# Order of the attention heads of the first half in an encoder layer: block by block, or the pairs of two blocks alternating

## Chip, cores and metric

The kernel runs on one core of a Trainium2 chip, in one launch. The metric is the time of one execution on the device in microseconds (us), as the median of several runs. The engines are named TensorE (PE in the rows; PEld is its weight load), VectorE (DVE), ScalarE (ACT), GpSimd (POOL) and SyncE (SP), whose queue starts nearly all DMA transfers here.

## The reference

One layer over 2048 positions of 1024 channels, all in float32:

```python
h = rms_norm(x, norm_mix_g[l])
z = h @ w_in[l]                      # u_a, v_a, q_b, k_b, v_b, f_logit
out_a = spatial_gating(u_a, v_a, ...)        # 8 heads, GELU and a layernorm per head
out_b = forgetting_attention(q_b, k_b, v_b, f_logit)   # 8 heads of 64
x = x + concatenate([out_a, out_b], -1) @ w_out[l]
x = x + conv_ffn(rms_norm(x, norm_ffn_g[l]), ...)
return rms_norm(x, norm_final_g)
```

`forgetting_attention` is causal: for head h and query t it takes `softmax(q k^T / 8 + c[t] - c[s])` over the keys s <= t, with c a running sum of log-sigmoids, and multiplies by v.

## The kernel before

The 2048 positions are four blocks of 512 queries, `tb` 0 to 3; blocks 0 and 1 are the first half. Every product is made in three matmuls from high and low parts of its operands (`mm3`, lines 180 to 192).

The order of the stages is: projections of the first half (`a_half(0)`: keys and queries, values, then `gated`, which has a layernorm stage of eight tiles and a gate stage of eight tiles, each tile 24 matmuls of `mm3`), projections of the second half (`a_half(1)`: the two `gated` stages first, then values, then keys and queries), the output projection of the first half (`c_half`), its feed-forward part (`d_half`), and the second half (`late_half`).

Attention is no stage of its own. It is a generator, `b_stream` (line 623), that takes a list of pieces (head, block) and makes them in that order. A piece has two parts. `b_max` (line 666) loads the queries t1 and t2, makes the scores of 128 queries against up to 512 keys in two matmuls (L686, L687), takes their row minimum (scores are stored negated) on VectorE (L690 for full blocks, L692 with the mask for the block on the diagonal), and the exponential with its sum on ScalarE (L695); it ends with the reciprocal of the sum (L714, or L716 in block 0). `b_mix` (line 726) makes the transposed scores (L747, L748), the mask (L751, diagonal only), the exponential (L753), a high and a low part of it (L758, L759) and the product with the values (L735, L736); it ends with L770 and L771, and after the second head of a pair the sums are turned to rows (L776), multiplied in and stored to `mixh[tb]` and `mixl[tb]` in DRAM (L782 to L785). `b_stream` runs the maxima of piece p+1 before the mixing of piece p. The score tiles are three banks in turn.

Every `yield` of the generator is one step. In block 0 `b_max` has 4 steps and `b_mix` 4, plus 2 that drain the last products, plus one in every odd head; in block 1 it is 8 and 8, plus the same. `start_fill` (line 464) starts the stream as the first half's values are done. `tick` (line 83), called after each matmul of a projection, adds 1 to a credit and makes one step for each 3.5 ticks in the first half, 4.0 in the second (`RATES`). Instructions of the stream are given a higher priority than what stands around them, and a list scheduler that knows estimated durations fixes each engine's final order when the program is built; each engine then runs its queue in order. Blocks 2 and 3 begin only when `self.ready` is set, after `phase_a`.

`need(tb)` (line 116) makes steps at once, without matmuls of a projection in between, until block `tb` is complete. `need(0)` stands in `a_half(1)` (line 430), after the first block's queries, ahead of `load_mix(0)`, which loads what attention and the gates of block 0 left in `mixh[0]` and `mixl[0]`; `need(1)` stands in `c_half` (line 810).

Of the kernel before, what the change touches and what calls it, by code (L numbers as in the profile page):

```python
# [31 lines left out]
RATES = [3.5, 4.0, 4.4, 3.6]  # L32
# [36 lines left out]
class Block:  # L69
# [45 lines left out]

    def need(self, tb):

        while self.done < 8 * (tb + 1):
            self.step()
            self.count += 3  # L120
            while self.late and self.late[0][0] <= self.count:
                self.late.pop(0)[2]()
# [262 lines left out]
    def a_half(self, half):  # L385
# [28 lines left out]
        def keys_queries():  # L414
            u0, u1 = self.first if half == 0 else (self.a_unit("k", 0), self.a_unit("k", 1))
            self.a_forget(half, 0)
            channels("k", 0, *u0, 0)
            channels("k", 1, *u1, 0)
            self.a_forget(half, 1)
            channels("k", 0, *u0, 1)  # L420
            channels("k", 1, *u1, 1)
            groups = (("k", (2, 3)), ("q", (0, 1)), ("q", (2, 3))) if half == 0 else (("k", (2, 3)), ("q", (0, 1, 2, 3)))
            for kind, cs in groups:
                with self.tc.issue_after(self.rows_ins), self.tc.issue_after(self.pow_ins):
                    us = [(c, self.a_unit(kind, c)) for c in cs]
                for b in range(2):
                    for c, u in us:
                        channels(kind, c, *u, b)
                    if half == 1 and kind == "q" and b == 0:
                        self.need(0)  # L430
                        self.mix0 = self.load_mix(0)

            if half == 0:
                with self.tc.issue_after(self.raw_ins):
                    self.a_gate_w(sp, pp)
                    self.scales = [self.a_rows(1, b, False) for b in range(2)]

        def values():
            for t, ps in token_major(2048):
                pv = ps.rearrange("p (h d) -> p h d", h=8)  # L440
                hl = self.til(sp, [P, 2, 8, 64], F32R, "vn")
                hi, lo = hl[:, 0, :, :], hl[:, 1, :, :]
                nc.scalar.activation(hi, pv, AF.Copy)
                nc.vector.tensor_tensor(lo, pv, f32(hi), op=ALU.subtract)
                self.dma(self.vd[half][t * P:(t + 1) * P, :, 0:64], f32(hi))
                self.dma(self.vd[half][t * P:(t + 1) * P, :, 64:128], f32(lo))

        def gated():
            vns = []
            for t, ps in token_major(512):  # L450
                if t % 2 == 0:
                    vns.append(self.til(sp, [P, 2, TB], F32, "vn"))
                self.a_layernorm(ps, vns[-1][:, t % 2, :])
            for t, ps in token_major(0):
                if t % 2 == 0:
                    self.a_mixed(vns[t // 2])
                self.a_gate(half * 2 + t // 4, t % 4, ps, vns[t // 2][:, t % 2, :])
                if half == 0 and t % 4 == 3:
                    self.a_norm(1, t // 4, self.scales[t // 4], 14 if t == 3 else 16, 9 if t == 3 else 6)

        if half == 0:
            keys_queries()
            values()
            self.start_fill(self.b_stream([(h, tb) for tb in range(4) for h in range(8)]), RATES[0])
            gated()
        else:
            self.rate = RATES[1]
            gated()
            values()
            keys_queries()  # L470
# [934 lines left out]
```

## Time and profile before

| | |
|---|---|
| median of 3 runs | 2499.26 us (2495.81 to 2500.54) |
| profiled execution, its own time | 2500.66 us |
| its span, first to last instruction | 2499.0 us |
| TensorE busy in the span | 2438.5 us, 98% |
| VectorE busy | 1743.9 us, 70% |
| ScalarE busy | 1365.2 us, 55% |
| GpSimd busy | 344.3 us, 14% |
| granted TensorE clock, mean | 0.995 of full speed |

The rows come from one profiled execution. Busy time is the time in which at least one instruction of an engine ran. An idle time is put down to the engine or transfer whose event ended it; of several events, to the last.

### The profile page before, as it was taken

To read this page: it belongs to the slowest core of one execution; us is meant where nothing else is said; L and a number is where in the kernel's file an instruction comes from. 1 tells how busy PE (TensorE), PEld (TensorE's weight loads), DVE (VectorE), ACT (ScalarE), POOL (GpSimd) and SP (SyncE) were. 2 spreads that over 40 slices of the span, in tenths; PEclk is the share of its full clock that TensorE was granted. 3 is DMA by queue.
4 is the path that set the end of the run, shared out by engine and by line. 5 is a ranking of instruction groups with operands and counts; after the bars stand their busy time and mean duration, and the time that the engine had idled before them with its cause. 6 is when DMAs were issued, how large, how long until landed. Compare 5 with 4: busy or idle time off the path is not lost.

```text
span 2499.0 us, 32991 instructions
## 1 busy us (share of the span) xinstructions
PE 2438.5 (98%) x11082; PEld 1995.1 (80%) x11082; DVE 1743.9 (70%) x3106; ACT 1365.2 (55%) x2629; POOL 344.3 (14%) x351
## 2 busy tenths in 40 slices
PE   8999989999999999999999999999999999999998
PEld 5787867878788888887888888878888887888887
DVE  5237667655457867887777875488788887857776
ACT  4327767654345556766676772255555545444443
POOL 3214122000014221121111121120000000001000
PEclk9999999999999999999999999999999999999999
DMA  6863543666857545554555545512222228538633
GB/s 181 260 165 101 160 120 113 186 163 179 281 186 239 161 144 167 185 173 154 170 160 154 180 154 197 165 43 93 81 80 82 84 80 299 168 102 293 196 119 122
DMA packets 346101, 396.08 MB, mean 158 GB/s; under 512 B 52908, under 2 KB 222068, under 8 KB 344508
## 3 DMA queue, kind: packets, MB, share of 16 engines
q1 hardware_dynamic: 340892, 369.85, 48.3%
q0 software_dynamic: 5040, 24.12, 2.5%
q8 instruction: 88, 1.44, 0.3%
q14 instruction: 81, 0.66, 0.1%
HBM read 300.30 MB, written 93.72 MB: 158 GB/s over the span
## 4 chain that ended last, share of the span: by engine, by line
PE 83%; DVE 5%; DMA 4%; ACT 4%; issue 2%; POOL 1%; SPq 1%; DVEq 0%; POOLq 0%; ACTq 0%
PE D L1271 15%; PE mm L188 12%; PE mm L190 12%; PE mm L192 12%; PE A L1085 3%; PE A L1084 3%; PE A L1086 3%; PE o L736 2%; PE o L735 2%; PE s L687 2%; PE s L686 2%; PE s L748 2%; PE s L747 2%; PE B L1084 2%; PE B L1085 2%
## 5 line engine op out<-in xcount | busy, mean ns | idle before, releaser
L188 PE MATMUL mm<-thi,whi 128*128 128x512 f32 x960 | 377.5, 393 | 2.7 <-DVE vn L398 2.7
L192 PE MATMUL mm<-thi,wlo 128*128 128x512 f32 x960 | 377.0, 393 | 0.1
L190 PE MATMUL mm<-tlo,whi 128*128 128x512 f32 x960 | 376.5, 392 | 0.0
L188 PE MATMUL mm<-whi,thi 128*128 128x512 f32 x640 | 253.5, 399 | 4.7 <-DVE m L704 1.1
L190 PE MATMUL mm<-wlo,thi 128*128 128x512 f32 x640 | 254.2, 397 | 1.8 <-DVE wlo L142 1.7
L192 PE MATMUL mm<-whi,tlo 128*128 128x512 f32 x640 | 252.9, 396 | 0.0
L130 POOL TENSOR_SCALAR whi<-raw 128x1024 fp32r<-128x1024 f32 x108 | 125.2, 1160 | 916.8 <-PE mm L190 514.2
L695 ACT ACTIVATE s<-s,part 128x512 f32<-128x512 f32 (+3 forms) x257 | 150.4, 585 | 147.5 <-DVE part L690 83.0
L188 PEld LDWEIGHTS mm<-thi,whi 128*128 128x128 f32 x960 | 180.5, 188 | 41.1 <-DVE vn L398 2.9
L192 PEld LDWEIGHTS mm<-thi,wlo 128*128 128x128 f32 x960 | 180.5, 188 | 38.4 <-DVE wlo L142 0.6
L190 PEld LDWEIGHTS mm<-tlo,whi 128*128 128x128 f32 x960 | 180.5, 188 | 37.2
L759 DVE TENSOR_TENSOR pl<-e,ph 128x512 fp32r<-128x512 f32 (+2 forms) x212 | 138.1, 658 | 62.2 <-ACT ph L758 34.4
L142 DVE TENSOR_TENSOR wlo<-raw,whi 128x1024 fp32r<-128x1024 f32 x108 | 135.2, 1253 | 47.6 <-POOL whi L130 47.3
L753 ACT ACTIVATE e<-s 128x512 f32<-128x512 f32 (+2 forms) x227 | 115.5, 528 | 72.4 <-DVE s L751 41.5
L188 PEld LDWEIGHTS mm<-whi,thi 128*128 128x128 f32 x640 | 121.4, 190 | 30.4 <-POOL whi L130 3.3
L190 PEld LDWEIGHTS mm<-wlo,thi 128*128 128x128 f32 x640 | 121.4, 190 | 27.1 <-DVE wlo L142 4.2
L1271 PE MATMUL D<-wl,xh 128*128 128x512 f32 x368 | 141.2, 389 | 0.0
L1271 PE MATMUL D<-wh,xh 128*128 128x512 f32 x368 | 140.8, 389 | 0.2 <-DVE xo L1343 0.2
L192 PEld LDWEIGHTS mm<-whi,tlo 128*128 128x128 f32 x640 | 121.2, 190 | 24.0
L758 ACT ACTIVATE ph<-e 128x512 fp32r<-128x512 f32 (+2 forms) x212 | 117.0, 561 | 39.5 <-PE o L735 31.5
L1271 PE MATMUL D<-wh,xl 128*128 128x512 f32 x368 | 138.0, 389 | 0.0
L690 DVE TENSOR_REDUCE part<-s 128x1 f32<-128x512 f32 x144 | 94.7, 682 | 20.4 <-PE s L687 19.9
(1864 smaller groups left out, 5845.0 us busy)
## 6 DMA issues: line engine op xcount, KB each, us to landing
raw<-in_w_up_dram SPq DMA_DIRECT2D x72, 512.0 KB
m<-kx SPq DMA_DIRECT2D x133, 256.0 KB
m<-kx SPq DMA_DIRECT2D x160, 136.0 KB
x<-act SPq DMA_DIRECT2D x84, 256.0 KB
raw<-in_w_in_dram SPq DMA_DIRECT2D x40, 512.0 KB
v<-vd SPq DMA_DIRECT2D x66, 256.0 KB
x<-in_x_dram SPq DMA_DIRECT2D x24, 512.0 KB
raw<-in_w_out_dram SPq DMA_DIRECT2D x24, 512.0 KB
```

The costliest lines, as they stand in the source:

```text
L130: self.cast_ins = self.nc.gpsimd.tensor_scalar(out, in_, 1.0, 0.0, ALU.mult, ALU.add).ins
L142: nc.vector.tensor_tensor(lo, raw, f32(hi), op=ALU.subtract)
L188: mm(ps, lhsT=ah[k], rhs=bh[k], start=k == 0, stop=False)
L190: mm(ps, lhsT=ah[k], rhs=bl[k], start=False, stop=False)
L192: mm(ps, lhsT=al[k], rhs=bh[k], start=False, stop=k == n - 1)
L695: nc.scalar.activation(ps[:, :n], ps[:, :n], AF.Exp, scale=-1.0, bias=dst, accum_out=ls[:, tt, sb:sb + 1])
L753: nc.scalar.activation(e[:, c], ps[:, c], AF.Exp, scale=-1.0)
L758: nc.scalar.activation(ph[:, c], e[:, c], AF.Copy)
L759: nc.vector.tensor_tensor(pl[:, c], e[:, c], f32(ph[:, c]), op=ALU.subtract)
L1084: mm(ps, lhsT=xh[:, ks], rhs=yh[:, k, :], start=fresh and k == 0, stop=False, **kw)
L1085: mm(ps, lhsT=xh[:, ks], rhs=yl[:, k, :], start=False, stop=False, **kw)
L1271: nc.tensor.matmul(bank[t], lhsT=x[i][:, ts], rhs=w[k], start=fresh and j == 0 and i + k == 0, stop=last and i == 1, **kw)
```

## The change

The list of pieces of the stream is written out. Before, it was all eight heads of block 0, then all of block 1, then of blocks 2 and 3. Now heads come in pairs: pair 0 of block 0, pair 0 of block 1, pair 1 of block 0, pair 1 of block 1, pairs 2 and 3 of block 0, pairs 2 and 3 of block 1, and then blocks 2 and 3 as before. `need` no longer counts eight heads for each block, but makes steps until the last piece that belongs to block `tb` or an earlier one is complete: 12 pieces for block 0, and 16, 24 and 32 for the others, as before.

```diff
     def need(self, tb):
 
-        while self.done < 8 * (tb + 1):
+        while self.done <= max(i for i, p in enumerate(self.pieces) if p[1] <= tb):
             self.step()
...
         if half == 0:
             keys_queries()
             values()
-            self.start_fill(self.b_stream([(h, tb) for tb in range(4) for h in range(8)]), RATES[0])
+
+            order = [(0, 0), (0, 1), (1, 0), (1, 1), (2, 0), (3, 0), (2, 1), (3, 1)]
+            order += [(pair, tb) for tb in (2, 3) for pair in range(4)]
+            self.pieces = [(2 * pair + i, tb) for pair, tb in order for i in range(2)]
+            self.start_fill(self.b_stream(self.pieces), RATES[0])
             gated()
```

## Rows read from the trace of the kernel before

**Rows 1.** The page: the span, the busy time of each engine in the whole span with its share and number of instructions, and TensorE's busy tenths in 40 equal slices of the span.

```profile
span 2499.0 us, 32991 instructions
PE 2438.5 (98%) x11082; PEld 1995.1 (80%) x11082; DVE 1743.9 (70%) x3106; ACT 1365.2 (55%) x2629; POOL 344.3 (14%) x351
...
PE   8999989999999999999999999999999999999998
```

**Rows 2.** Busy time by stage, one row for each stretch: its ends and length, the busy time (and number of instructions) of PE, PEld, DVE, ACT and POOL, the granted clock of TensorE, the mean busy share of the DMA engines, and GB/s. The stretches are, in order, the layernorm and the gate stage of the first half, the same two of the second half, the second half's values, and its keys and queries.

```profile
187.00:250.00 63.00, 57.45 (x267) 46.82 (x266) 47.34 (x104) 45.80 (x74) 25.01 (x18) 0.97 0.35 103
250.00:330.00 80.00, 72.62 (x389) 60.17 (x388) 51.10 (x119) 54.83 (x99) 16.30 (x22) 0.98 0.57 171
330.00:400.00 70.00, 65.33 (x317) 52.56 (x316) 53.80 (x116) 54.61 (x95) 24.96 (x17) 1.00 0.30 88
400.00:475.00 75.00, 71.82 (x364) 58.99 (x364) 49.29 (x105) 55.46 (x98) 10.07 (x7) 1.00 0.51 146
475.00:530.00 55.00, 55.00 (x256) 44.10 (x255) 27.79 (x56) 24.45 (x57) 3.15 (x3) 1.00 0.75 188
530.00:656.00 126.00, 126.00 (x583) 101.29 (x581) 69.09 (x159) 62.90 (x142) 8.42 (x8) 1.00 0.71 207
```

**Rows 3.** Waits of TensorE, longest in total first: who waited for whom, us in total, times, longest. The first five rows are of the stretch from 187 to 330 us, the last three of that from 330 to 475 us (in whose list no wait for queries, t<-qx, stands).

```profile
PE s L687 <- DMA t<-qx: 1.8, 2, 1.2
PE s L686 <- DMA t<-qx: 1.6, 1, 1.6
PE s L747 <- ACT e L753: 1.6, 1, 1.6
PE s L747 <- ACT s L695: 1.5, 2, 0.8
PE s L686 <- ACT s L695: 1.3, 1, 1.3
...
PE s L686 <- ACT s L695: 1.8, 3, 0.9
PE s L163 <- ACT e L753: 1.7, 1, 1.7
PE s L747 <- DMA m<-kx: 1.1, 1, 1.1
```

**Rows 4.** Groups of instructions by line on ScalarE, four of the stretch from 187 to 330 us and then the same four of that from 330 to 475 us: count, busy us and mean ns of one, idle time before them.

```profile
L758 ACT ACTIVATE ph<-e 128x512 fp32r<-128x512 f32 (+3 forms) x24 | 10.8, 469 | 0.3
...
L695 ACT ACTIVATION_READ_ACCUMULATOR s<-s,part 128x1 f32 x21 | 4.1, 196 | 0.0
L770 ACT ACTIVATE op<-o 64x512 f32<-64x512 f32 x6 | 3.6, 592 | 3.0 <-PE o L736 2.8
...
L776 ACT ACTIVATE rw<-rr 128x512 f32<-128x512 f32 x3 | 1.9, 627 | 0.2 <-DVE rr L716 0.2
...
L758 ACT ACTIVATE ph<-e 128x512 fp32r<-128x512 f32 (+3 forms) x24 | 13.0, 549 | 2.4 <-DVE pl L759 2.0 <-ACT ph L758 0.2
...
L695 ACT ACTIVATION_READ_ACCUMULATOR s<-s,part 128x1 f32 x31 | 6.2, 199 | 0.0
L770 ACT ACTIVATE op<-o 64x512 f32<-64x512 f32 x3 | 1.8, 592 | 0.1
L776 ACT ACTIVATE rw<-rr 128x512 f32<-128x512 f32 x2 | 1.3, 631 | 0.9 <-DVE rr L714 0.9
```

**Rows 5.** Two groups with the times of their first and last start: the ends of heads (L771) that lie between 366 and 528 us, which are the first four of block 1, and the loads of combined blocks between 300 and 660 us.

```profile
L771 DVE TENSOR_TENSOR op<-o,op x4: 682/688/695, 413.1 to 526.0; 64x512 f32<-64x512 f32 x4
...
L88 SPq DMA_DIRECT2D thi<-mixh x7: 376/471/621, 623.4 to 656.2; - x7
```

**Rows 6.** Groups of ScalarE from 187 to 475 us with the shapes kept apart: the widest and the narrowest form of the three operations of a step, and the split at the end of a pair.

```profile
L695 ACT ACTIVATE s<-s,part 128x512 f32<-128x512 f32 x25 | 16.5, 659 | 4.7 <-DVE part L690 4.6
L758 ACT ACTIVATE ph<-e 128x512 fp32r<-128x512 f32 x21 | 13.1, 628 | 0.3 <-ACT ph L758 0.2
...
L753 ACT ACTIVATE e<-s 128x512 f32<-128x512 f32 x22 | 12.8, 592 | 6.0 <-DVE s L751 4.3 <-PE s L748 1.3
...
L176 ACT ACTIVATE ph<-op 128x512 fp32r<-128x512 f32 x5 | 3.1, 629 | 0.0
...
L695 ACT ACTIVATE s<-s,part 128x128 f32<-128x128 f32 x9 | 3.0, 333 | 1.2 <-DVE part L692 1.2
L758 ACT ACTIVATE ph<-e 128x128 fp32r<-128x128 f32 x9 | 2.8, 308 | 0.2
L753 ACT ACTIVATE e<-s 128x128 f32<-128x128 f32 x9 | 2.5, 277 | 6.6 <-DVE s L751 6.5
```

**Rows 7.** Two stretches of 10 us, columns as in group 2.

```profile
220.00:230.00 10.00, 10.00 (x45) 8.45 (x44) 6.83 (x18) 6.99 (x14) 4.31 (x3) 0.86 0.35 106
...
320.00:330.00 10.00, 7.27 (x30) 5.35 (x30) 4.83 (x9) 4.58 (x8) 1.85 (x4) 0.83 0.73 224
```

**Rows 8.** Loads of ScalarE's function tables from 187 to 475 us, by the line of the instruction that follows (L695 and L753 exponential, L488 and L506 Gelu).

```profile
L695 ACT ACT_TABLE_LOAD x21 | 26.9, 1283 | 3.4 <-DVE part L690 1.6 <-DVE part L692 1.5
...
L488 ACT ACT_TABLE_LOAD x16 | 20.5, 1283 | 0.3
...
L506 ACT ACT_TABLE_LOAD x15 | 19.2, 1283 | 0.4 <-PE mm L192 0.2
L753 ACT ACT_TABLE_LOAD x10 | 12.8, 1283 | 0.2
```

## The prediction

> **What bounds the kernel now.** I read the page's engine shares first [rows 1]. TensorE is busy for 2438.5 us of a span of 2499.0 us, so at most 60.5 us can be won by filling it better; the row of tenths shows its few eights in the first fifth. Then the stages around the change, each in one stretch [rows 2]. The stream of attention steps runs there beside projections that keep TensorE supplied. TensorE is idle for 63 - 57.45 = 5.55 us in the layernorm stage of the first half, 80 - 72.62 = 7.38 us in its gate stage, 70 - 65.33 = 4.67 us and 75 - 71.82 = 3.18 us in the same two stages of the second half: 20.8 us in 288 us. In the values, keys and queries that follow it is busy for all of 55 and 126 us. So an attention step is paid for, beyond its matmuls, only between 187 and 475 us; after that it is free, and the sum of the matmuls is the same in any order. ScalarE is the busiest other engine there (45.80 of 63, 54.83 of 80, 54.61 of 70, 55.46 of 75 us), and the waits of TensorE [rows 3] name it most often: part of the stalls is matmuls of attention that wait for an exponential to free a score bank or to make weights, part is a load of queries.
>
> **Where the stream stands in these stages.** A step is one yield of the stream. By the code a head of block 0 has 4 steps of maxima and 4 + 2 of mixing (one more for odd heads), 10.5 on average; a head of block 1 has 8 and 8 + 2 (+1), 18.5. The counts tell how many steps ran where [rows 4]: a maximum step leaves one accumulator read (L695), a mixing step one L758; a finished head leaves one L770 (and two steps of draining), a finished pair one L776 (and one step). From 187 to 330 us that is 21 + 24 + 2 x 6 + 3 = 60 steps; from 330 to 475 us 31 + 24 + 2 x 3 + 2 = 63. Before 187 us there were 18 (three heads' maxima and one mixing). So these stages hold steps 18 to 141 of 232. Going through the old order, these 123 steps are 66 of block 0 (59 in the first stretch, 7 in the second) and 57 of block 1. In the new order the same 123 places hold 53 of block 0 (21 and 32) and 70 of block 1 (39 and 31). I assume that the stream advances at the same pace in steps, since nothing else in the emission changes.
>
> **The change, part by part.**
>
> Removed and added instructions: none. The same 16 heads with the same widths, loads, maxima and stores are emitted; both orders have 12 heads (eight of block 0, four of block 1) in their first 12 places and the same head in place 16, so everything from there on stands where it stood.
>
> The test in `need`: it asks for 12 heads instead of 8 before block 0's output is read. It costs nothing if 12 are done by then. In emission they are: 384 matmuls at 3.5 per step and 896 at 4.0 give 109 + 224 = 333 steps before `need(0)`, and head 12 is mixed at step 166. On the chip step 166 is, in the old order too, the end of the fourth head of block 1, at 526.0 us, and the first load of the combined block 0 is issued at 623.4 us [rows 5]: 97 us of cover. If that cover were gone, each further us of delay would reach the output projection in full.
>
> Idle time per step. The first stretch lost 12.93 us in 60 steps, 0.216 us each, nearly all of block 0. In the second, 7.85 us less 7 steps at 0.216 leaves 6.34 us for 56 steps of block 1, 0.113 us each. If the loss belongs to the kind of step, 13 fewer of block 0 and 13 more of block 1 save 13 x 0.103 = 1.3 us. If it belongs to the stage, it is 0. One can see why the kind may matter: a step of block 1 brings wider matmuls for one chain of the same length, and fewer heads begin per step (a head's start needs fresh queries; the loads cost 1.8 + 1.6 us in the first stretch and none in the second [rows 3]). I take 1.3 us, as the two rates come from stages with the same projections.
>
> ScalarE. Its time per step, from the widths [rows 6]; the widths between 512 and 128 lie on the line between them. Block 0, maxima: 4 x ((0.659 + 0.333)/2 + 0.197) = 2.77 us; mixing: 4 x ((0.592 + 0.277)/2 + (0.628 + 0.308)/2) = 3.61 us; end of a head 0.592 and half a pair's 0.628 + 0.629, together 1.22 us: 7.60 us in 10.5 steps, 0.72 us a step. Block 1 adds 4 full maxima, 4 x 0.856 = 3.42 us, and 4 full mixings, 4 x 1.22 = 4.88 us: 15.9 us in 18.5 steps, 0.86 us. The first stretch gets 38 steps more of block 1, 38 x 0.14 = 5.3 us more ScalarE work in 143 us that already hold 100.6 us; the second gets 25 fewer, 3.5 us less in 145 us with 110.1 us. Net 1.8 us of exponentials move forward from the stages where they are free. As long as the share stays near 74%, I cost this at 0: what hides it is the projection's matmuls, which wait for nothing of attention but stand in the same queue. The bounds are -3.5 us (only the relief of the second stretch counts) and +5.3 us (every us of the first is waited for).
>
> Clock. From 320 to 330 us the granted clock was 0.83, a mixture of 1.2 and 2.4 GHz, right behind waits for queries, in a stretch where TensorE was busy 7.27 of 10 us; from 220 to 230 us it was 0.86 [rows 7]. That is 1.7 and 1.4 us lost. The first dip stands at the beginning of the ninth head's maxima (step 77). In the new order step 77 lies inside a head, so I count half of that dip as gone, 0.8 us, with 0 and 3.1 us as the bounds.
>
> The DMA queue: the same loads, 13 for a head of block 1 in 18.5 steps against 8 in 10.5. Fewer starts in the first stretch (4 after step 18 instead of 6), and more in the second, where queries are not waited for at all. It is contained in the rate per step; alone it would be two starts of six, at 3.4 us for six 1.1 us.
>
> Sum: -1.3 - 0.8 = -2.1 us. The profiled execution took 2500.66 us (span 2499.0 us and 1.66 us around it), 1.4 us above the median of 2499.26 us, so against its own time 2498.6 us, and as a median **2497.2 us**. A measurement of this kernel can tell about 0.2% from no change, 5.0 us; the runs before spread over 4.7 us. So the forecast is no measurable change: stalls are handed round, and a us or two goes.
>
> **The rivals.**
>
> *Faster: the mixture fills the gaps.* A wide step of block 1 next to a narrow one gives TensorE work while ScalarE catches up, so that half the 20.8 us and half of the two dips vanish: 10.4 + 1.6 = 12 us, 2487 us. For it: the lower loss per step of block 1, and that ScalarE has less to do for each column of block 1 (0.86 us a step for 416 columns on average, 0.72 us for 320). Against: the order in which engines get work is fixed long before, and within a head the steps are as before; only every second head boundary joins two blocks. Chance 0.22. The Trainium skill ("Perfetto Trace Analysis", "Optimization Strategy") speaks for this one: it advises interleaving regimes when the most contended engine changes over time. The busy shares of [rows 2] do change by stage, but only between attention stages and projections; by steps of either block ScalarE's need differs by a fifth.
>
> *Slower: ScalarE becomes what the first half waits for.* Block 1's exponentials now stand among the Gelus of the first layernorm and gate stages. Price: the 5.3 us of the first stretch are waited for, and the second stretch gives nothing back because its 32 steps of block 0 lose 0.216 us each (25 x 0.103 = 2.6 us more). 5.3 + 2.6 = 7.9 us, 2507 us. It decides from the point where TensorE's waits for L695 and L753 in the first stretch, 1.6 + 1.5 + 1.3 = 4.4 us now, exceed about 9 us. Against: ScalarE is idle for 42 of the 143 us. Chance 0.17. The waits come in bursts around table loads: 21 + 16 + 15 + 10 = 62 of them at 1.283 us, 79.5 us of ScalarE in 288 us [rows 8]; both orders put exponentials between the same 32 Gelus, so I keep their number. The Trainium skill ("ScalarE: Activation LUTs", "Rules for kernel authors") says to do all of one table set before switching and to budget 2.7 us a switch; neither order groups. Eight loads more or fewer would be 10 us of ScalarE by the rows' duration and 21 us by the page's budget.
>
> *Late output of block 0.* The last pair of block 0 slips past 623 us, and the projection waits. It needs 97 us of slip. Chance 0.03, 2510 us and above.
>
> *Nothing at all.* The loss belongs to the stage: 2499 us. It is inside the forecast's own range, 2493 to 2503, which holds 0.50 with it. The remaining 0.08 are other placements of the whole queue, either way.
>
> **How the numbers follow.** Faster by over 0.2%: the faster rival's 0.22, 0.06 from the lower edge of the forecast and half of the remainder, 0.32. Slower: 0.17 and 0.03, less what falls inside 0.2%, plus the other half, 0.21. Same 0.47. The range reaches to both rivals, 2486 to 2508.
>
> **What would show it.** Right: idle of TensorE from 187 to 475 us within 17 to 23 us, the first stretch down by about 3 us, the second up by about 2; about 60 steps in the first stretch, now mostly 512 wide; values and queries still without idle. The dip at 320 us gone says that half of my clock term was right. Wrong: idle under 12 us (the faster rival); waits for L695 and L753 over 9 us before 330 us with ScalarE above 85% (the slower one); the load of block 0 after 650 us; or a difference that lies behind 710 us, where the two programs should be alike.

## The result

Measured side by side, the kernel before took 2499.16 us (median of 14 runs, 2495.08 to 2502.36) and the changed one 2502.31 us (14 runs, 2497.31 to 2507.13): a ratio of 1.0018, with a 95% interval of 1.001 to 1.0026. The change costs about 3 us where the prediction saw a gain of 2.1. The time lies in the predicted range (2486 to 2508), and under 0.2%, but the interval excludes no change: the sign was wrong. Taken together, 25 runs of the new order (these 14 and r2 below) have a mean of 2502.64 us, and 93 runs of the old order, those that stood beside the experiments below, one of 2500.05 us.

The profiled execution took 2503.41 us, its span is 2501.4 us. Lines from 465 on have moved by 4: L690 of the new kernel is L686 of the old, L699 is L695, L751 is L747, L757 is L753, L492 is L488. The page of the new kernel answers [rows 1]:

```profile
span 2501.4 us, 32992 instructions
PE 2443.8 (98%) x11082; PEld 1997.8 (80%) x11082; DVE 1747.3 (70%) x3106; ACT 1363.8 (55%) x2629; POOL 345.5 (14%) x351
```

TensorE executes the same 11082 matmuls, but is busy for 5.3 us longer. Its idle time in the span has even fallen, from 60.5 to 57.6 us. So some of them ran slower. Next, the busy times by stage, in the stretches and columns of [rows 2] and one behind them (the output projection's beginning), for the new kernel:

```profile
187.00:250.00 63.00, 57.68 (x259) 46.06 (x258) 44.32 (x101) 45.83 (x80) 25.45 (x18) 0.97 0.29 89
250.00:330.00 80.00, 76.61 (x411) 63.96 (x409) 54.41 (x124) 57.08 (x104) 14.44 (x20) 1.00 0.59 178
330.00:400.00 70.00, 65.44 (x312) 52.36 (x312) 50.18 (x114) 58.77 (x101) 24.11 (x18) 0.98 0.31 92
400.00:475.00 75.00, 71.84 (x363) 59.75 (x362) 48.37 (x112) 52.68 (x92) 12.07 (x9) 0.95 0.50 150
475.00:530.00 55.00, 52.73 (x250) 43.70 (x249) 28.07 (x59) 21.16 (x52) 3.52 (x4) 1.00 0.71 183
530.00:656.00 126.00, 126.00 (x583) 99.94 (x582) 69.18 (x158) 62.32 (x139) 9.48 (x9) 1.00 0.72 207
656.00:710.00 54.00, 50.55 (x220) 40.07 (x219) 28.54 (x54) 20.11 (x49) 6.90 (x7) 0.97 0.70 239
```

The last of these rows as it was in the kernel before:

```profile
656.00:710.00 54.00, 49.87 (x214) 40.38 (x214) 26.77 (x52) 18.23 (x43) 6.98 (x8) 0.94 0.70 230
```

The idle time of the four stages around the attention steps is 5.32 + 3.39 + 4.56 + 3.16 = 16.4 us, 4.4 us less than the 20.8 us of [rows 2]; the gate stage of the first half alone gives 4.0. Against it stand 2.27 us in the second half's values, which had no idle time before. The other change is in the granted clock, of which the prediction had not thought that it could fall in new places: it is below 1.00 in four of the seven stretches (before in three), and 0.95 from 400 to 475 us, where it was 1.00 [rows 2].

### The profile page after: what moved, and what is told of

The parts are those of the page before. It is cut to its first block, busy times and chain, and to the rows that moved or that the text cites. A ratio compares the mean times of both kernels' runs of the same rounds, so it can differ in the third digit from the quotient of the medians.

```text
span 2501.4 us, 32992 instructions
## 1 busy us (share of the span) xinstructions
PE 2443.8 (98%) x11082; PEld 1997.8 (80%) x11082; DVE 1747.3 (70%) x3106; ACT 1363.8 (55%) x2629; POOL 345.5 (14%) x351
## 4 chain that ended last, share of the span: by engine, by line
PE 89%; DMA 3%; DVE 3%; ACT 2%; POOL 1%; issue 1%; SPq 0%; POOLq 0%; DVEq 0%; ACTq 0%
PE D L1275 17%; PE mm L188 13%; PE mm L190 13%; PE mm L192 13%; PE A L1089 3%; PE A L1088 3%; PE A L1090 3%; PE o L740 2%; PE o L739 2%; PE s L691 2%; PE s L751 2%; PE s L752 2%; PE s L690 2%; PE B L1088 2%; PE B L1089 2%; PE B L1090 2%
## 5 line engine op out<-in xcount | busy, mean ns | idle before, releaser
L188 PE MATMUL mm<-thi,whi 128*128 128x512 f32 x960 | 377.8, 394 | 2.6 <-DVE vn L398 2.6
L190 PE MATMUL mm<-tlo,whi 128*128 128x512 f32 x960 | 377.7, 393 | 0.0
L192 PE MATMUL mm<-thi,wlo 128*128 128x512 f32 x960 | 377.4, 393 | 0.2 <-DVE wlo L142 0.2
L188 PE MATMUL mm<-whi,thi 128*128 128x512 f32 x640 | 254.1, 400 | 5.4 <-ACT u L492 4.6
L190 PE MATMUL mm<-wlo,thi 128*128 128x512 f32 x640 | 254.7, 398 | 1.5 <-DVE wlo L142 1.5
L192 PE MATMUL mm<-whi,tlo 128*128 128x512 f32 x640 | 252.8, 396 | 0.0
L699 ACT ACTIVATE s<-s,part 128x512 f32<-128x512 f32 (+3 forms) x257 | 150.8, 587 | 142.5 <-DVE part L694 96.5
L188 PEld LDWEIGHTS mm<-thi,whi 128*128 128x128 f32 x960 | 180.9, 188 | 41.3 <-DVE vn L398 2.9
L192 PEld LDWEIGHTS mm<-thi,wlo 128*128 128x128 f32 x960 | 180.9, 188 | 38.5 <-DVE wlo L142 0.7
L190 PEld LDWEIGHTS mm<-tlo,whi 128*128 128x128 f32 x960 | 180.8, 188 | 38.2
L757 ACT ACTIVATE e<-s 128x512 f32<-128x512 f32 (+2 forms) x227 | 115.9, 528 | 87.7 <-DVE s L755 42.2
L188 PEld LDWEIGHTS mm<-whi,thi 128*128 128x128 f32 x640 | 121.7, 190 | 31.6 <-ACT u L492 5.6
L190 PEld LDWEIGHTS mm<-wlo,thi 128*128 128x128 f32 x640 | 122.0, 191 | 26.9 <-DVE wlo L142 3.7
L192 PEld LDWEIGHTS mm<-whi,tlo 128*128 128x128 f32 x640 | 121.6, 190 | 24.3
L694 DVE TENSOR_REDUCE part<-s 128x1 f32<-128x512 f32 x144 | 94.8, 683 | 26.4 <-PE s L691 25.9
```

Of the source, the lines that this page charges most:

```text
L188: mm(ps, lhsT=ah[k], rhs=bh[k], start=k == 0, stop=False)
L190: mm(ps, lhsT=ah[k], rhs=bl[k], start=False, stop=False)
L192: mm(ps, lhsT=al[k], rhs=bh[k], start=False, stop=k == n - 1)
L699: nc.scalar.activation(ps[:, :n], ps[:, :n], AF.Exp, scale=-1.0, bias=dst, accum_out=ls[:, tt, sb:sb + 1])
```

## Where the clock falls in the new order

Three stretches of 10 us, same columns; a stretch of 10 us at 0.83 loses 1.7 us to the lower of the two levels (1.2 and 2.4 GHz), one at 0.66 loses 3.4 us:

```profile
190.00:200.00 10.00, 7.56 (x28) 5.80 (x27) 3.81 (x13) 8.58 (x17) 0.00 (x0) 0.83 0.40 128
330.00:340.00 10.00, 9.22 (x41) 7.66 (x42) 4.33 (x11) 8.44 (x14) 1.80 (x3) 0.83 0.36 103
415.00:425.00 10.00, 8.53 (x32) 6.86 (x32) 3.59 (x9) 7.25 (x10) 0.67 (x1) 0.66 0.25 69
```

The waits of TensorE in the same kernel, as in [rows 3]: first from 187 to 330 us, then from 330 to 475 us, and the last two from 475 to 720 us.

```profile
PE s L751 <- DMA m<-kx: 2.4, 1, 2.4
PE mm L188 <- ACT u L492: 1.3, 1, 1.3
...
PE mm L188 <- ACT u L492: 3.3, 2, 1.8
PE s L751 <- ACT s L699: 1.5, 1, 1.5
...
PE s L690 <- DMA t<-qx: 2.3, 1, 2.3
PE s L751 <- DMA m<-kx: 2.0, 1, 2.0
```

The longest waits of [rows 3] were for queries and exponentials, 1.2 to 1.7 us each. Now one is for keys (2.4 us, it ends at 194.5 us), and in three the projection itself, at L188, waits for a Gelu (1.3 us at 259 us, then two that end at 331 and 417 us), 4.6 us in all. Before, it did so once from 187 to 475 us:

```profile
PE mm L188 <- ACT u L488: 0.7, 1, 0.7
```

How that comes about is seen where the clock falls for longest. TensorE and then ScalarE in the timeline of the new kernel: start, duration, engine, line, instruction, and in brackets the idle time before it and who ended it.

```profile
414.59 0.51 PE L740 MATMUL o<-pl,v 128*128 128x512 f32 x1 [0.95 <-DVE pl L763]
...
416.74 0.79 PE L188 MATMUL mm<-whi,thi 128*128 128x512 f32 x1 [1.47 <-ACT u L492]
417.33 0.63 PE L190 MATMUL mm<-wlo,thi 128*128 128x512 f32 x1
417.76 0.63 PE L192 MATMUL mm<-whi,tlo 128*128 128x512 f32 x1
```

```profile
413.98 0.38 ACT L757 ACTIVATE e<-s 128x256 f32<-128x256 f32 x1 [1.73 <-DVE s L755]
414.26 0.52 ACT L762 ACTIVATE ph<-e 128x384 fp32r<-128x384 f32 x1
414.80 1.28 ACT L492 ACT_TABLE_LOAD   x1
416.09 0.60 ACT L492 ACTIVATE u<-mm 128x512 f32<-128x512 f32 x1
```

ScalarE takes these in the order of its queue. An exponential of a diagonal block waits for its mask (1.73 us, L755 on VectorE), and the Gelu that frees the projection's bank stands behind it, with a table load of 1.28 us between. TensorE has waited for 0.95 and 1.47 us, within 3.1 us, when it goes on, and then its matmuls start 0.59 and 0.43 us apart, where at the full clock the same ones start 0.33 and 0.24 us apart (below, in e7). In this execution not only the 2.4 us of waiting are lost, but also the clock behind it.

## Experiments

The theories before the runs. **A, the clock:** the new order puts waits of TensorE close together, in other places than the old one, and the granted clock falls behind them; that takes what the better filling gives. **B, the wait for keys:** the 2.4 us at 194 us, with its clock, are the cost. **C, the values stage:** block 0 now ends with the sixth pair, so that its last steps press the second half's values (the wait of 2.3 us at 488 us). Other rivals stand in the expectations.

Two numbers are compared throughout: the mean granted clock of all runs of a kernel (0.001 of it is 2.5 us if every us at half speed counts, "at full count" below; among the 93 runs of the old order, 0.001 of the listed clock goes with 1.6 us of the time), and, of its one profile, idle time plus time lost at half speed between 187 and 710 us (half the length of the stretches in which 1.2 GHz was granted, taken from the times at which the grant changes). The medians of the kernel before in the three comparisons are 2499.69, 2498.82 and 2500.81 us, so a ratio says more than a median. The ratios with their intervals are those on record; the plain ratios of the medians differ from them by up to 0.0008 (after 1.0013, e7 1.0008, e10 0.9954), which is not small beside the differences between the orders.

| run | median us (runs) | ratio to before, 95% | mean clock | idle + lost at half speed, 187 to 710 us |
|---|---|---|---|---|
| before | 2499.16 (14) | 1 | 0.9952 (93 runs) | 24.9 + 6.8 = 31.7 |
| after | 2502.31 (14) | 1.0018 [1.001, 1.0026] | 0.9936 | 22.1 + 8.5 = 30.7 |
| r1 need only | 2498.78 (11) | 0.9997 [0.9988, 1.0006] | 0.9958 | 25.8 + 1.7 = 27.6 |
| r2 new again | 2502.42 (11) | 1.001 [1.0001, 1.0019] | 0.9943 | 21.1 + 8.5 = 29.7 |
| e1 late mix | 2497.76 (11) | 0.9994 [0.9985, 1.0003] | 0.9950 | 20.3 + 5.1 = 25.5 |
| e2 early mix | 2496.76 (11) | 0.9981 [0.9972, 0.999] | 0.9953 | 21.8 + 3.4 = 25.2 |
| e3 Gelu first, new | 2501.46 (11) | 1.0006 [0.9997, 1.0015] | 0.9942 | 20.2 + 6.8 = 27.0 |
| e4 Gelu first, old | 2501.57 (11) | 1.0009 [0.9998, 1.002] | 0.9942 | 22.0 + 5.1 = 27.1 |
| e5 late and early | 2493.26 (11) | 0.9974 [0.9965, 0.9983] | 0.9940 | 17.9 + 8.5 = 26.4 |
| e6 full mix | 2502.21 (11) | 1.001 [1.0001, 1.0019] | 0.9952 | 22.4 + 5.1 = 27.5 |
| e7 three places busy | 2502.87 (12) | 1.0004 [0.9995, 1.0013] | 0.9959 | 19.2 + 5.1 = 24.3 |
| e8 one place busy | 2501.89 (12) | 1.0005 [0.9996, 1.0015] | 0.9948 | 21.0 + 6.8 = 27.8 |
| e9 busy elsewhere | 2509.86 (9) | 1.0032 [1.0021, 1.0042] | 0.9936 | 23.2 + 10.2 = 33.5 |
| e10 e5, its places busy | 2489.38 (6) | 0.9946 [0.9934, 0.9958] | 0.9967 | 10.2 + 0.0 = 10.2 |

The column on the right comes from one execution, and executions of one kernel differ by some us in it (31.7 and 27.6 for the old order, 30.7 and 29.7 for the new); the mean clock is the firmer number. By that column alone the new order is hardly worse than the old: 30.2 against 29.7 us, as means of two profiles each.

### r1 and r2: the parts of the change

r1 has the new test in `need` and the old order; r2 is the changed kernel once more.

```diff
-            order = [(0, 0), (0, 1), (1, 0), (1, 1), (2, 0), (3, 0), (2, 1), (3, 1)]
+            order = [(0, 0), (1, 0), (2, 0), (3, 0), (0, 1), (1, 1), (2, 1), (3, 1)]
```

> The new test in need with the old order of pieces: the instructions of the kernel before, so 1.000 and about 2499 us by every theory. It gives a second profile of the old order with the granted clock. Theory A (the clock): the old order shows about 2 dips of the granted clock between 150 and 710 us, the new one 4 or more, and each dip of 3.4 us at half speed costs 1.7 us; the extra dips carry most of the 3 to 4.5 us. Theory B (the start): what is lost is the wait for keys at 194 us that the first head of block 1 brings, 2.4 us, and the dip at once with it, 1.7 us. Theory C (the end): block 0's heads now stand in the stage of the second half's values, which had no idle time, and lose 2.3 us there.

> The changed kernel once more, for a second profile and more times: 1.0018 by every theory. Theory A: four or more dips between 150 and 710 us again. Theory B: the wait for keys near 194 us again, over 1.5 us. Theory C: the wait for queries near 489 us again, over 1.5 us. A wait that doesn't come back in the second profile is chance.

The test alone changes nothing that can be told (0.9997), and the whole change costs again (1.001). So the loss belongs to the order. r2 also shows that the pattern repeats: the waits of B (1.94 us at 190 us) and C (2.30 us at 485 us) are there again, and the profile has idle time of 9.5 and 6.3 us in the two stretches (after: 8.7 and 7.7), and a clock of 0.98 and 0.97 there.

```profile
187.00:330.00 143.00, 133.48 (x655) 108.73 (x654) 96.05 (x218) 103.50 (x180) 41.53 (x40) 0.98 0.45 137
330.00:475.00 145.00, 138.74 (x689) 113.49 (x688) 100.59 (x231) 111.22 (x194) 34.23 (x23) 0.97 0.43 127
```

The same two rows of r1, with the old order: more idle time, and the full clock (in the kernel before, 0.97 and 0.98 in the first two stages [rows 2]). A had expected some two falls in r1; there is one from 187 to 710 us, at 658 us.

```profile
187.00:330.00 143.00, 129.48 (x661) 106.09 (x660) 100.23 (x223) 102.32 (x175) 40.66 (x40) 1.00 0.48 143
330.00:475.00 145.00, 137.28 (x683) 111.92 (x682) 102.50 (x220) 110.29 (x195) 34.78 (x24) 1.00 0.41 120
```

### e1 and e2: other mixtures

e1 puts the second pair of block 0 ahead of the first of block 1, and block 0 still ends with the sixth pair. e2 begins as the new order, with block 1 second, and block 0 ends with the fifth pair.

```diff
-            order = [(0, 0), (0, 1), (1, 0), (1, 1), (2, 0), (3, 0), (2, 1), (3, 1)]
+            order = [(0, 0), (1, 0), (0, 1), (2, 0), (1, 1), (3, 0), (2, 1), (3, 1)]   # e1
+            order = [(0, 0), (0, 1), (1, 0), (2, 0), (3, 0), (1, 1), (2, 1), (3, 1)]   # e2
```

> Order of pairs (pair, block): 00 10 01 20 11 30 21 31: the first four heads are all of block 0, as before; the alternation begins later, and block 0 still ends with the sixth pair, in the stage of values. Theory B (the start): no wait at 194 us, 0.9995 to 1.0005. Theory C (the end): the loss stays, 1.0015 to 1.002. Theory A: follows the count of dips, 1.7 us for each beyond the old order's.

> Order of pairs: 00 01 10 20 30 11 21 31: one pair of block 1 early, all of block 0 done by the fifth pair, before the values of the second half. Theory B (the start): the wait at 194 us stays, 1.0015 to 1.002. Theory C (the end): gone, 0.9995 to 1.0005. Theory A: follows the count of dips.

B falls: e2 keeps a wait of 1.99 us for the keys, with the clock falling behind it at 192 us, and is faster than the old order all the same (0.9981). C falls as the main cause: e1 has block 0 end as late as the new order, and idle time in the values and what follows (2.7 us from 475 to 656 us), and isn't slower (0.9994). Mixing the blocks isn't bad in itself; e2's loss at half speed is 3.4 us against the new order's 8.5.

### e3 and e4: the Gelu ahead of the exponentials

The Gelu of the layernorm stage gets the priority of the stream, in the new order (e3) and in the old (e4).

```diff
-        nc.scalar.activation(u, pu, AF.Gelu)
+        with self.tc.high_priority(AHEAD_B):
+            nc.scalar.activation(u, pu, AF.Gelu)
```

> The new order, with the Gelu of the gates at the priority of the attention stream, so that the projection's next tile doesn't wait behind exponentials. In both profiles of the new order TensorE waits 4.5 us for that Gelu in three places (0.7 us once in the old order), and the dips at 328 and 413 us begin there. Theory A (waits at the stage borders, doubled by the clock): the waits for the Gelu fall under 1.5 us, the dips near 328 and 413 us go, 9 us of half-speed loss between 187 and 710 us become 4 to 5 us, ratio 0.997 to 0.999. Rival D (the dips are chance, or come with any rearranged queue): time and mean clock stay, 1.001 to 1.002.

> The old order with the same Gelu priority. Theory A: it has little to gain, since its waits for this Gelu are 0.7 us and its dips few: 0.9995 to 1.001. Rival D: any rearranged queue costs or gains as much, 0.998 to 1.003. Together with the run before it: if the Gelu is what made the new order slower, new less old is 0 or below here, against 0.001 to 0.0018 without it.

Between the two the order makes no difference any more (2501.46 and 2501.57 us), which A had expected, but not in the way that it had expected: e3 missed its gain, and the old order lost about as much as the new one gained, though neither is clear of its interval. TensorE's waits for a Gelu fell only from 4.6 to 3.4 us in e3, and the clock still fell in four places. In e4 the mean clock fell to the new order's level (0.9942), by 0.0013 or 3.2 us below the old order in the same comparison (0.9955). But the edit moves more than the Gelu: the list scheduler arranged all queues anew, and in e4's trace over 1000 of TensorE's 11082 matmuls stand in another place than in r1's. So the pair doesn't decide between A and the rival D of the expectations, by which any rearranged queue can cost as much.

### e5 and e6: two more orders

e5 joins the beginning of e1 to the end of e2; e6 alternates throughout, so block 0 ends with the seventh pair.

```diff
-            order = [(0, 0), (0, 1), (1, 0), (1, 1), (2, 0), (3, 0), (2, 1), (3, 1)]
+            order = [(0, 0), (1, 0), (0, 1), (2, 0), (3, 0), (1, 1), (2, 1), (3, 1)]   # e5
+            order = [(0, 0), (0, 1), (1, 0), (1, 1), (2, 0), (2, 1), (3, 0), (3, 1)]   # e6
```

> Order of pairs 00 10 01 20 30 11 21 31: only one pair of block 1 is moved, to the third place. Theories B and C taken singly have already failed (the wait at 194 us stayed in e2 and it was faster; block 0 ended late in e1 and it was not slower). Theory A: follows the sum of idle time and half-speed loss from 187 to 710 us, which was 29.5 us in the old order (two profiles), 30.8 in the new, 25.3 in e1 and in e2: a profile with a sum under 27 us has a ratio under 1.000, one over 30 a ratio over 1.000.

> All four pairs alternate: 00 01 10 11 20 21 30 31, block 0 done after 14 heads, about step 203 of 232. Theory A: as for e5, by the sum of idle time and half-speed loss. If block 0's output comes too late (the prediction's deadline), the first load of the combined block 0 moves behind 650 us and the idle time from 656 us on grows from 3 to 4 us to over 8 us: 1.002 and more.

e5 is the best order of heads (0.9974). Its idle time is the lowest, 17.9 us, but its clock is as low as the new order's (0.9940): a fall of the clock doesn't make an order slow by itself, it is one of two terms. Its sum, 26.4 us, is below A's mark of 27, and its ratio below 1, as A had it. e6 is as slow as the new order (1.001) with a mean clock like the old one's (0.9952). Its sum from 187 to 710 us, 27.5 us, lies between the marks that A had set (below 27 faster, above 30 slower), so it is no evidence for either; and the clock doesn't explain it. Nor does a late block 0: from 656 to 710 us, where the output projection begins, its idle time is 2.7 us against 4.1 of the old order, and the first load of the combined block is issued at 622.6 us, before the mark of 650.

e6 shows one thing more. Its first five pairs are those of the new order, and in the two traces TensorE has the same matmuls in the same order up to 449 us. The waits are the same too: 1.78 us for the Gelu at 328 us, and the close pair that stood before the longest fall. But here the clock stays at its full level behind them. The two matmuls of e6 that wait, with those that follow the second, and a stretch of 10 us around them:

```profile
412.06 0.50 PE L740 MATMUL o<-pl,v 128*128 128x512 f32 x1 [0.95 <-DVE pl L763]
...
414.21 0.51 PE L188 MATMUL mm<-whi,thi 128*128 128x512 f32 x1 [1.46 <-ACT u L492]
414.55 0.40 PE L190 MATMUL mm<-wlo,thi 128*128 128x512 f32 x1
414.79 0.40 PE L192 MATMUL mm<-whi,tlo 128*128 128x512 f32 x1
```

```profile
412.00:422.00 10.00, 8.47 (x45) 7.11 (x46) 3.94 (x12) 9.87 (x16) 1.15 (x1) 1.00 0.41 123
```

So these waits don't bring a fall every time. In after and r2 there were three falls from 187 to 449 us, in e6 only the first, at 191 us; this is one execution, but the mean clock over e6's runs (0.9952 against 0.9939) agrees with it. And e6 is as slow as the new order without those falls, which speaks against A as the whole cause, unless its later part costs as much in another way. In the same way the wait of 2.3 us for queries near 486 us has no fall behind it in after, r2 and e8, and one in e7 and e9. What decides, these runs don't show; in all the profiles, though, each fall from 187 to 710 us stands at a wait of TensorE or begins within 2.1 us of the end of one.

### e7, e8 and e9: TensorE kept busy before the waits, and elsewhere

These leave every queue as it is in the new kernel; in the traces TensorE's order of matmuls is the new kernel's but for the copies. Once the schedule is fixed, some matmuls are issued several times in place, each copy writing the same result over itself: in e7 8 times L690 ahead of the wait at 190 us, 10 times L751 ahead of that at 327 us, 16 transposes (L163, 128 columns) ahead of those at 411 and 413 us (times as in r2); in e8 the 16 transposes alone; in e9 8, 8 and 16 of the same lines at 556, 577 and 588 us, where TensorE waits for nothing.

```diff
+            line, n = {'I-1785': (690, 8), 'I-2760': (751, 10), 'I-3588': (163, 16)}.get(ins.name, (0, 0))   # e7
...
+            for k in range(n + 1):
+                sync = s and type(s)(on_wait=list(s.on_wait) if k == 0 else [], on_update=list(s.on_update) if k == n else [])
+                out.append(type(ins)(name=nc.get_next_instruction_name() if k else ins.name, sync_info=sync,
+                                     stop_tensor_calc=True if k < n else ins.stop_tensor_calc, **kw))
```

> The new order with the same queues of all engines, except that 34 matmuls of TensorE are made again, right behind their originals and into the same place, just ahead of three waits that stand before dips of the clock: 8 of L690 ahead of the wait for keys at 190 us, 10 of L751 ahead of the wait for the Gelu at 327 us, 16 transposes (L163) ahead of the waits at 411 and 413 us. They fill about 1.8 us each. Theory A (the clock carries the loss): the dips at 190 and 327 us and the long one at 412 us go (1.7 + 1.7 + 3.4 us of loss), the added work falls into idle time, new less 4 to 6 us: 0.9985 to 0.9995, mean clock 0.9955 or more. Rival E (the waits themselves are the loss, the clock only goes with them): the added work costs nothing and gains nothing, or adds up to 1 us: 1.001 to 1.002.

> As e7, with the 16 transposes ahead of the waits at 411 and 413 us alone. Theory A: the long dip at 412 us goes, 3.4 us less than the new order: 0.999 to 1.0005. Rival E: 1.001 to 1.002.

> The price of such added matmuls where TensorE has no wait: 8 of L690 at 556 us, 8 of L751 at 577 us and 16 transposes at 588 us, the new order otherwise. 16 x 0.23 + 16 x 0.11 = 5.4 us if nothing hides them, so 1.0032 to 1.004 by both theories; dips as in the new order.

In e7 the clock stays at its full level in all three places; the same three stretches of 10 us as above:

```profile
190.00:200.00 10.00, 9.40 (x42) 7.33 (x41) 5.38 (x21) 7.53 (x12) 1.64 (x1) 1.00 0.17 48
330.00:340.00 10.00, 9.36 (x49) 7.38 (x48) 6.96 (x18) 8.37 (x16) 0.73 (x1) 1.00 0.45 126
415.00:425.00 10.00, 10.00 (x60) 8.77 (x60) 5.73 (x15) 8.38 (x14) 0.00 (x0) 1.00 0.32 86
```

And the same matmuls of TensorE in the timeline: the 16 copies and the four transposes that were there before (x20) stand ahead of L740, which no longer waits; the wait for the Gelu is shorter, and behind it L188, L190 and L192 start 0.33 and 0.24 us apart.

```profile
409.63 2.35 PE L163 MATMUL s<-ident,rw 128*128 128x128 f32 x20
411.74 0.48 PE L740 MATMUL o<-pl,v 128*128 128x512 f32 x1
...
413.32 0.50 PE L188 MATMUL mm<-whi,thi 128*128 128x512 f32 x1 [0.93 <-ACT u L492]
413.65 0.40 PE L190 MATMUL mm<-wlo,thi 128*128 128x512 f32 x1
413.89 0.39 PE L192 MATMUL mm<-whi,tlo 128*128 128x512 f32 x1
```

e8 takes away the long fall at 412 us and leaves those at 193 and 330 us. These are single executions, and e6 lacks two of the falls without any copies; firmer are the mean clocks of the runs, 0.9939 in the new order, 0.9948 in e8 and 0.9959 in e7. So the copies, place by place, do raise the clock: that much is shown. The gain in time that A expected did not come: e7's ratio (1.0004) lies between what A and its rival E expected, and its mean of 2502.64 us is that of the new order. e8 (1.0005) is at the upper edge of what A expected, and its interval holds much of E's range too. A gives two reasons for e7: the 34 copies are only partly hidden (some 5.4 us of work, while the idle time from 187 to 475 us fell by 3.1 us against r2), and the clock now falls at 483 us too and for longer at 675 us, from 656 to 710 us to 0.94. That the time did not rise by the 2 us between is what speaks for A here, but the intervals are nearly as wide.

```profile
656.00:710.00 54.00, 50.10 (x212) 39.89 (x211) 26.89 (x51) 19.53 (x47) 8.46 (x10) 0.94 0.67 229
```

The cleaner comparison is e7 with e9, which have 34 and 32 copies of the same lines, some 5.4 us of work in each, and are 7.1 us apart in the mean (2502.64 and 2509.70 us, in one comparison). Their mean clocks, 0.9959 and 0.9936, are worth 5.9 us at full count and 3.8 us by the 1.6 us for 0.001; their idle times from 187 to 710 us (23.2 and 19.2 us) are another 4.0 us. Together that is 7.8 to 9.9 us, so the two terms account for the difference, though the share of each isn't told. The same work costs 7 us less where it covers the waits.

### e10: e5 with its own waits covered

The order of e5, and the copies ahead of its four worst waits (20 times L483, 14 times L163, 8 times L188, 14 times L690, at 243, 328, 390 and 665 us).

```diff
+            line, n = {'I-2430': (483, 20), 'I-3386': (163, 14), 'I-4237': (188, 8), 'I-6385': (690, 14)}.get(ins.name, (0, 0))
```

> The order of e5 (0.9974) with added matmuls ahead of its own four waits that stand before dips: 20 of L483 at 243 us, 14 transposes at 328 us, 8 of L188 at 390 us, 14 of L690 at 665 us (there the wait for keys is 3.4 us). Theory A: 0.9945 to 0.996, since its profile loses 8.5 us by the clock between 187 and 710 us. Rival E: 0.997 to 0.998.

The ratio is 0.9946, inside what A expected: the fastest of all, 11 us under the old order's median in the same comparison and faster than e5 by more than either's interval, although it executes 56 matmuls more than e5. Here the terms can be added up. The copies are 34 of 128 columns at 0.11 us and 22 of 512 columns at 0.23 us, 8.8 us of work; the idle time from 187 to 710 us fell by 7.7 us; and the mean clock rose by 0.0027, 6.7 us at full count and 4.3 us by the 1.6 us for 0.001. That makes -3.2 to -5.6 us. The means, each against the old order's in its own comparison, differ by -4.8 us, the ratios by -7 us. Filling the waits alone would not have made it faster, since the copies are longer than the idle time that went. The rows of e5, then of e10, from 187 to 330, 330 to 475 and 656 to 710 us:

```profile
187.00:330.00 143.00, 134.71 (x675) 111.53 (x673) 97.86 (x221) 106.25 (x182) 39.14 (x37) 0.99 0.46 137
330.00:475.00 145.00, 139.37 (x696) 116.01 (x697) 106.10 (x232) 106.02 (x190) 36.53 (x28) 0.98 0.47 138
...
656.00:710.00 54.00, 50.02 (x214) 40.13 (x213) 25.92 (x51) 18.96 (x46) 8.05 (x10) 0.94 0.69 228
```

```profile
187.00:330.00 143.00, 137.75 (x722) 115.02 (x720) 97.94 (x222) 108.31 (x187) 42.46 (x40) 1.00 0.47 138
330.00:475.00 145.00, 140.34 (x714) 116.72 (x715) 105.31 (x232) 105.14 (x187) 34.13 (x24) 1.00 0.47 137
...
656.00:710.00 54.00, 53.69 (x245) 43.71 (x244) 27.03 (x53) 20.93 (x52) 9.91 (x13) 1.00 0.74 240
```

No stretch is below 1.00 any more. From 656 to 710 us TensorE is busy for 3.7 us more (some 3.2 us of it the 14 copies of L690), and at the full clock.

## Why the prediction failed

**The step that failed is the clock term.** The prediction took -0.8 us with bounds of 0 and 3.1 us of gain; it counted what the old order's two falls cost, and let them stay or go, but not that the new order makes falls of its own. From 187 to 710 us half speed cost 6.8 and 1.7 us in the two profiles of the old order and 8.5 us in both of the new. Over 25 runs the new order's mean clock is 0.99388, against 0.99516 in 93 runs of the old: 0.0013 of 2500 us, +3.2 us at full count, where -0.8 us was forecast. That the clock goes with the difference is also seen without any profile: where runs of the new order list the same clock as runs of the old, their mean times are near each other (at 0.995 2500.9 and 2500.2 us, at 0.994 2502.2 and 2502.1, at 0.993 2504.0 and 2504.8; at 0.996, with two runs of the new order, 2499.4 and 2497.9); the new order has its runs at the lower values. A line through all 118 runs with one slope for both orders leaves 0.5 us between them (standard error 0.6), so by it the lower clock goes with 2.1 of the 2.6 us. That copies ahead of the waits raise the clock is shown by e7, e8 and e10; that the clock is worth time is shown by e10 against e5 and, in part, by e7 against e9. That it is the whole of the loss is not shown, and e6 speaks against it: the same beginning, the old order's clock, and still 2.3 us slower than the old order in the mean. The sum over the terms does not close either: with the idle time of the whole span down by 3.2 us (60.5 and 58.9 us in two profiles of the old order, 57.6 and 55.5 in two of the new) and the clock at +3.2 us the time should have stayed, and it rose by 2.6 us. The gain in idle time does not show in the time. The records can't place it: TensorE's busy time less what half speed costs in it comes out at 2425.1 and 2428.7 us for the old order and at 2426.8 and 2429.2 us for the new, so it differs by 3.6 us between two executions of the same work. In these four profiles alone the spans do add up (-3.2 us of idle time, +5.2 us of clock, +1.1 us of that rest, together +3.1 us), but the two of the old order had a higher clock (0.9946 and 0.9972) than its runs on average.

**The rate per step** (-1.3 us: -3 in the first stretch, +2 in the second) was right in sign and too small: -4.9 us was measured, as the mean of two profiles of each order. From 187 to 330 us the idle time went from 12.94 (13.52 in r1) to 8.71 (9.52 in r2) us, -4.1 on average; from 330 to 475 us, where a rise was forecast, from 7.85 (7.72) to 7.72 (6.26) us, -0.8. The sum of the two, 16.4 and 15.8 us, lies just below the 17 to 23 us that were called right. The loss belongs neither to the block of a step nor to the stage alone: some 38 more steps of block 1 in the first stretch went with less of it, and some 25 more of block 0 in the second did not bring more.

**The pace of the stream** held. The counts of [rows 4] in the new kernel, two rows from 187 to 330 us and two from 330 to 475 us:

```profile
L762 ACT ACTIVATE ph<-e 128x512 fp32r<-128x512 f32 (+3 forms) x24 | 12.2, 524 | 1.9 <-PE o L739 0.9 <-DVE pl L763 0.6
L699 ACT ACTIVATION_READ_ACCUMULATOR s<-s,part 128x1 f32 x30 | 5.9, 197 | 0.0
...
L762 ACT ACTIVATE ph<-e 128x512 fp32r<-128x512 f32 (+3 forms) x28 | 14.2, 513 | 3.2 <-DVE lns L513 1.9 <-PE o L739 1.1
...
L699 ACT ACTIVATION_READ_ACCUMULATOR s<-s,part 128x1 f32 x24 | 4.8, 199 | 0.0
```

With 4 and 5 ends of heads and 2 of pairs in each, that is 30 + 24 + 8 + 2 = 64 steps and 24 + 28 + 10 + 2 = 64, where there were 60 and 63.

**"After that it is free"**, of the stages from 475 us on, was wrong by 2.3 us: TensorE waits for queries of the stream (2.3 us at 488 us), where the old order's profile had no idle time from 475 to 656 us, and r1 1.1 us.

**The late output of block 0** doesn't happen, as predicted. The ends of heads between 366 and 528 us, and the first load of the combined block, in the columns of [rows 5]:

```profile
L775 DVE TENSOR_TENSOR op<-o,op x6: 674/688/695, 398.3 to 521.6; 64x512 f32<-64x512 f32 x6
...
L88 SPq DMA_DIRECT2D thi<-mixh x7: 415/467/1940, 628.4 to 659.4; - x7
```

The twelfth head ends at 521.6 us, and the load is issued at 628.4 us: 107 us of cover, and 5 us later than before, inside the marks.

**ScalarE.** The slower rival had the sign and the engine, but not the mechanism. By its own marks it fell: ScalarE is busy for 45.83 + 57.08 = 102.9 of 143 us, 72% (85% was the mark), 2.3 us more than before where 5.3 were expected, and TensorE's waits for L699 and L757 from 187 to 330 us are 1.1 + 1.0 + 0.8 + 0.3 = 3.2 us, not above 9. In the waits above it is not the amount of exponentials that counts but what stands behind a waiting one: a Gelu, and behind that the projection. The prediction took ScalarE at 0 because the projection's matmuls "wait for nothing of attention"; through that queue they do, for 4.6 us where it was 0.7. The number of table loads, 62, stayed, as taken: 18 + 16 + 15 + 12 + 1, each of 1.28 us; in the timeline above the Gelu starts 0.01 us behind its load. The Trainium skill ("ScalarE: Activation LUTs", "Rules for kernel authors") budgets 2.7 us for a switch; this trace shows 1.3 us of it.

**The faster rival** had half of its case: alternating does fill the gaps, by 3 to 4 us here and by 7 in e5 (24.9 to 17.9 us from 187 to 710 us). The Trainium skill's advice on interleaving regimes ("Perfetto Trace Analysis", "Optimization Strategy") agrees with that. What the whole time makes of it depends on more than the idle time: e5, with the least of it, is the fastest order, and the new one is slower than the old.

**Open.** Why e6 is slow with the old order's clock; why the clock falls behind the same waits in one execution and not in another; where the new order's gain in idle time went; and why each order puts its waits where it does. The list scheduler rearranges every queue when the order of heads changes, and from the list of heads alone none of the six orders' times could have been told: they lie between 0.9974 and 1.0018 with no line through them that these runs show.

## What to carry to other kernels

On a kernel whose TensorE is busy for 98% of the time, compare the granted clock as well as the idle time: here 3 us less waiting came with 2 to 3 us of lost clock, and the time rose by 2.6 us, not all of which is explained. Waits of 1 to 2.4 us can cost more than their length here (after), but need not (e6), so one profile of a kernel isn't enough to judge them. Harmless repeated matmuls ahead of them can be cheaper than the waits (e10), while such repeats where nothing waits cost their full price (e9). When one list order gives 0.9974 and another 1.0018, a term below 0.2% isn't forecast from the list: try several, and see whether covering the waits that are left helps.

## What was not expected of the hardware

Adding work made the kernel faster: 56 more matmuls in e10 took the ratio from 0.9974 to 0.9946, with a mean granted clock of 0.9967 against 0.9940. And waits of TensorE of 0.95 and 1.47 us, within 3.1 us in a kernel that is otherwise saturated, were followed by a granted clock of 0.66 over 10 us (415 to 425 us), that is 3.4 us lost behind 2.4 us of waiting; with the repeated transposes of e7 ahead of them (20 records of L163 take 2.35 us, 16 of them copies) it stayed at 1.00. But it stayed at 1.00 in e6 as well, behind the same two waits and with no repeats.
